# Gated delta rule on one core: the halves of x ahead of the mask constants, a large clear later, and six filter panels computed with channels on the partitions

## The chip, the cores and the metric

The kernel runs on one core of a Trainium2 chip. The time is device microseconds of one execution, the median of several runs. The core has a matrix engine (PE, TensorE; its weight loads are shown apart as PEld), a vector engine (DVE), a scalar engine (ACT), GpSimd (POOL) and a queue engine (SP) that here mostly issues the loads.

## The reference, cut to what matters

The program is one block of a small model on 256 tokens of width 1024: a gated delta rule mixer, a feed-forward layer, an S5 mixer, two mixtures of experts and per-layer embeddings. Only the first is touched:

```python
def gdn_mixer(x, w_in, conv_w, a_log, dt_bias, norm_g, w_out):
    proj = x @ w_in                                       # 256 x 1024 by 1024 x 4112
    qkv, z, b, a = jnp.split(proj, [...], axis=-1)        # q, k, v, z of 1024 columns, b and a of 8
    qkv = jax.nn.silu(causal_dwconv(qkv, conv_w))         # 4 taps along the tokens, for each channel
    q = l2norm(q) * (GDN_DK ** -0.5); k = l2norm(k)       # 8 heads of 128
    beta = jax.nn.sigmoid(b)
    g = -jnp.exp(a_log) * jax.nn.softplus(a + dt_bias)
    o = gated_delta_rule_chunked(q, k, v, g, beta)        # needs the inverse of (I + L) in each chunk
    o = o * lax.rsqrt(jnp.mean(o * o, -1, keepdims=True) + NORM_EPS) * norm_g
    return (o * jax.nn.silu(z)).reshape(bsz, seq, GDN_V) @ w_out
```

## The kernel before, in words

**The projection.** x is turned to have its 1024 features on the partitions and split into two halves whose sum is x: ACT writes `xh` (the high half), DVE `xl` (what is left). w_in is loaded by SP in pieces of 1 MiB (`raw`, five buffers); each 128x1024 slice of a piece is split the same way into `hi` (ACT, line 182) and `lo` (DVE, line 196) in three buffers. A product is then three matmuls, hi times xh, lo times xh, hi times xl (lines 204 to 206). First come the 16 columns of b and a (`sp`, 256 columns wide), then eight panels of 512 columns in the order k0, k1, q0, q1, v0, v1, z0, z1. `dense` keeps x as the stationary operand and streams 512 columns of weights, so a panel is 48 matmuls 512 wide into two PSUM banks (`mm`, four buffers) with tokens on the partitions.

**The filter.** For the six panels of k, q and v (`conv4`) ACT copies both banks to `pr` (line 498), PE turns them by eight transposes (line 503) into `tr` banks with channels on the partitions, ACT scales a copy (`cv`, line 505), and DVE adds the three other taps (line 507, three of them for each of four channel tiles). The z panels are not filtered.

**The inverse.** From k's panels LT is made (line 526); its 16x16 diagonal blocks go by SP through DRAM to `B`, DVE solves them in 15 steps (lines 572 and 574) and copies the result (`X`, line 575), and SP spreads X over the block diagonal of `DD` (lines 577 and 582), which must have been cleared (line 532). Then PE, ACT and DVE double the size of the inverted blocks: for each of two halves, three levels and two quarters, PE forms a product (line 601), ACT copies it (`pb`, line 603), PE multiplies (line 611, at the last level 607), DVE writes it under a mask (`lm`, line 612 or 608) and, but for the last level, PE turns the result (line 615) for ACT to copy (line 616). Each step needs the one before. The masks are made from a bitwise xor of two index tiles (`fi`, `pi`, `xf`).

**Order.** The instructions of an engine run in the order in which the program lists them. That list is made by a scheduler from the written order and from priorities; each instruction waits for its data by semaphores. So the matmuls of later panels that the list has between two steps of the inverse are what PE does while it waits for ACT and DVE there. What comes behind the mixer (feed-forward, S5, experts) has the same order on every engine in both kernels, from w_out's product on.

Of the kernel before, what the change touches and what calls it, by code (L numbers as in the profile page):

```python
# [6 lines left out]
F32 = mybir.dt.float32  # L7
F32R = mybir.dt.float32r
U8 = mybir.dt.uint8
I32 = mybir.dt.int32  # L10
U32 = mybir.dt.uint32
AF = mybir.ActivationFunctionType
ALU = mybir.AluOpType
# [3 lines left out]
P = 128  # L17
D = 1024
NT = 2
KD = 8  # L20
# [41 lines left out]
def behind(tc, ins, first):  # L62

    tc.add_manual_dep(ins.ins, first.ins.name, mybir.DependencyInfo(mybir.DependencyClass.NoSync, mybir.DependencyReason.DATA), reason="order")
# [13 lines left out]
class Net:  # L78
# [129 lines left out]
    def dense(self, xh, xl, w, k0, kn, n0, n, ps, first=True, last=True, then=None, lag=0):  # L208
# [27 lines left out]
        for go in late:  # L236
            go(1)

    def to_T(self, xs, xh, xl, gain=None, kt=KD, view=None, pin=False):

        nc = self.nc
        T = Pinned(self.tc, nc.tensor) if pin else nc.tensor
        done = []
        for k in range(0, kt, 2):
            n = min(2, kt - k)
            ps = self.tr()
            for j in range(n):
                for b in range(NT):
                    T.transpose(ps[:, (j * 2 + b) * P:(j * 2 + b + 1) * P], xs[b][:, (k + j) * P:(k + j + 1) * P], self.ident)  # L249
            for j in range(n):  # L250
                sl = slice(k + j, k + j + 1)
                h, l = xh[:, sl, :], xl[:, sl, :]
                v = ps[:, j * 256:(j + 1) * 256]
                if view is not None:
                    h, l = view(h)[:, 0], view(l)[:, 0]
                    v = v.rearrange("p (b j s) -> p b j s", b=2, s=4)
                else:
                    h, l = h[:, 0], l[:, 0]
                if gain is None:
                    if view is None:  # L260
                        if j == 0:
                            m = slice(k, k + n)
                            a = ps[:, :n * 256].rearrange("p (a b) -> p a b", a=n)
                            c = nc.scalar.copy(xh[:, m, :], a)
                            d = nc.vector.tensor_tensor(out=xl[:, m, :], in0=a, in1=xh[:, m, :].bitcast(F32), op=ALU.subtract)
                            done.append((c, d))
                    else:
                        nc.scalar.copy(h, v)
                        nc.vector.tensor_tensor(out=l, in0=v, in1=h.bitcast(F32), op=ALU.subtract)
                else:  # L270
                    g = gain[:, sl]
                    nc.scalar.activation(h, v, AF.Copy, scale=g)
                    nc.vector.scalar_tensor_tensor(out=l, in0=v, scalar=g, in1=h.bitcast(F32), op0=ALU.mult, op1=ALU.subtract)
        return done
# [123 lines left out]
    def gdn(self, pool, xs, outs):  # L398
        nc, i = self.nc, self.i
        V, A, T, G = nc.vector, nc.scalar, nc.tensor, nc.gpsimd  # L400
        H = 8
        w = i["gdn_w_in"]

        def t(shape, name, dt=F32, bufs=1):
            return pool.tile(shape, dt, tag=name, name=self.nm(name), bufs=bufs)


        cw = t([P, 24, 4], "cw"); nc.scalar.dma_start(cw, i["gdn_conv_w"])
# [9 lines left out]
        mneg = t([P, P], "mneg")  # L418
        G.memset(mneg, 0.0)
        G.affine_select(out=mneg, in_=mneg, pattern=[[1, P]], compare_op=ALU.is_ge, fill=-1e30, base=0, channel_multiplier=-1)  # L420
        fi = t([P, P], "fi", I32); G.iota(fi, pattern=[[1, P]], base=0, channel_multiplier=0)
        pi = t([P, P], "pi", I32); G.iota(pi, pattern=[[0, P]], base=0, channel_multiplier=1)
        V.tensor_tensor(out=fi, in0=fi, in1=pi, op=ALU.bitwise_xor)
        xf = t([P, P], "xf"); V.tensor_copy(xf, fi)
        lm = t([P, 7, P], "lm", U8)
        for l in range(4, 7):
            V.tensor_scalar(out=pi.bitcast(F32), in0=xf, scalar1=float(1 << l), scalar2=None, op0=ALU.is_ge)
            V.scalar_tensor_tensor(out=lm[:, l, :], in0=xf, scalar=float(2 << l), in1=pi.bitcast(F32), op0=ALU.is_lt, op1=ALU.mult)
        i2 = t([40, H], "i2"); sel = t([40, H, P], "sel", F32R)
        V.tensor_tensor(out=i2, in0=self.ident[:40, 0:8], in1=self.ident[:40, 32:40], op=ALU.add)  # L430
        G.tensor_copy(sel, i2.unsqueeze(2).to_broadcast([40, H, P]))
# [2 lines left out]
        xh, xl = self.xT()  # L434
# [18 lines left out]
        s8 = slice(32, 40)  # L453
# [8 lines left out]
        p0 = self.tr()  # L462
# [3 lines left out]
        p0 = self.tr()  # L466
# [4 lines left out]
        p0 = self.tr()  # L471
        for b in range(NT):
            T.matmul(p0[0:8, b * P:(b + 1) * P], gt[:, b, :], tri, start=True, stop=True)
        rw = t([40, 256], "rw", F32R)
        G.memset(rw.bitcast(F32), 0.0)
        A.copy(rw[0:8], p0[0:8, :256])
        V.tensor_tensor(out=rw[s8], in0=p0[0:8, :256], in1=rw[0:8].bitcast(F32), op=ALU.subtract)

        qT = t([P, H, 256], "qT"); kT = t([P, H, 256], "kT")
        vb = self.zt().rearrange("p b (h d) -> p b h d", h=H)  # L480
# [1 line left out]
        p0 = self.tr()  # L482
# [4 lines left out]
        def panel(n0):  # L487
            ps = [self.mm() for _ in range(NT)]
            self.dense(xh, xl, w, 0, KD, n0, 512, ps)
            return ps  # L490

        def conv4(n0, dst):

            ps = panel(n0)
            pr = [t([P, 512], "pr", bufs=3) for _ in range(NT)]
            to = []
            for b in range(NT):
                A.copy(pr[b], ps[b])
            for j in range(4):
                ct = n0 // P + j  # L500
                pt = self.tr()
                for b in range(NT):
                    T.transpose(pt[:, b * P:(b + 1) * P], pr[b][:, j * P:(j + 1) * P], self.ident)
                cv = t([P, 256], "cv", bufs=4)
                A.activation(cv, pt[:, :256], AF.Copy, scale=cw[:, ct, 3:4])
                for d in range(1, 4):
                    V.scalar_tensor_tensor(out=cv[:, d:], in0=pt[:, :256 - d], scalar=cw[:, ct, 3 - d:4 - d], in1=cv[:, d:],
                                           op0=ALU.mult, op1=ALU.add)
                to.append(cv if dst is None else dst(j))
                A.activation(to[j], cv, AF.Silu)  # L510
            return to

        def sumsq(src, n, dst):

            ps = self.tr()
            for j in range(4):
                sq = t([P, 256], "sq", bufs=2)
                G.tensor_tensor(out=sq, in0=src[:, 4 * n + j, :], in1=src[:, 4 * n + j, :], op=ALU.mult)
                for b in range(NT):
                    T.matmul(ps[:, b * 4 + j:b * 4 + j + 1], sq[:, b * P:(b + 1) * P], ones[:, 0:1], start=True, stop=True)  # L520
            V.tensor_copy(dst[:, :, 4 * n:4 * n + 4], ps[:, :8].rearrange("p (b h) -> p b h", b=NT))
# [7 lines left out]
        E = t([P, H, 384], "E"); LT = t([P, H, 384], "LT")  # L529
        B = t([P, 16, 16], "B"); X = t([P, 2, 16, 16], "X"); tp = t([P, 16, 16], "tp")  # L530
        DD = t([P, 2, 16, P], "DD")
        G.memset(DD, 0.0)
        G.memset(X, 0.0)
        G.memset(X[:, 0].rearrange("p a b -> p (a b)")[:, 0:256:17], 1.0)
        if "s5_log_dt1" in i:
# [13 lines left out]
        for n in range(2):  # L549
# [14 lines left out]
            for r in range(8):  # L564
                s = slice(16 * r, 16 * r + 16)
# [5 lines left out]
        for r in range(1, 16):  # L571
            V.tensor_tensor(out=tp[:, 0:r, 0:r], in0=X[:, 0, 0:r, 0:r].rearrange("p j n -> p n j"),
                            in1=B[:, 0:r, r].unsqueeze(1).to_broadcast([P, r, r]), op=ALU.mult)
# [4 lines left out]
        for n in range(2):  # L578
            for r in range(8):
                s = slice(16 * r, 16 * r + 16)  # L580
# [48 lines left out]
        for n in range(2):  # L629
            vT = conv4(2048 + 512 * n, None)  # L630
            for j in range(4):
                h = 4 * n + j
                pt = self.tr()
# [5 lines left out]
        for n in range(2):  # L639
            ps = panel(3072 + 512 * n)  # L640
# [1402 lines left out]
```

## Time and profile before

| what | us |
|---|---|
| runs | 1688.21, 1681.74, 1687.71 |
| median | 1687.71 |
| profiled execution | 1682.82 |
| its span in the trace | 1681.1 |
| PE busy in the span | 1545.4 (92%) |
| DVE busy | 720.7 (43%) |
| ACT busy | 489.9 (29%) |

The span is the time from the first to the last instruction of the profiled execution; 1.7 us lie around it. The mixer is the first stage. The shares of busy time are averages over the whole program; in the mixer DVE is far busier than 43%.

### The profile page before, as it was taken

How to read it: one execution, taken by the hardware profiler on the slowest of the kernel's cores; microseconds unless marked ns; L12 is line 12 of the kernel's file. 1: busy time of each engine (PE TensorE's matmuls, PEld its weight loads, DVE VectorE, ACT ScalarE, POOL GpSimd, SP SyncE). 2: the span in 40 equal slices, each digit the busy share in tenths (PEclk: the TensorE clock that was granted, in tenths of full speed). 3: DMA queues.
4: the chain of work that ended last, by engine and by line, in shares of the span. 5: the costliest groups of instructions: out<-in, count | busy, mean ns of one | idle time of the engine just before them, and what ended most of it. 6: DMA issues, size and time to landing. Idle time of an engine off the chain costs nothing. (4 is left out here: it accounts for less than half of the span.)

```text
span 1681.1 us, 25494 instructions
## 1 busy us (share of the span) xinstructions
PE 1545.4 (92%) x10438; PEld 946.0 (56%) x10438; DVE 720.7 (43%) x1334; ACT 489.9 (29%) x821; POOL 293.8 (17%) x432
## 2 busy tenths in 40 slices
PE   7999987879978979999999997988999999999997
PEld 5778866667877944544445545874443343443436
DVE  6884678757677541111111117562322222222216
ACT  5565454335542521100101014451111111111116
POOL 2201169768364000000000004000000000000000
PEclk9999999889978979999999998998999999999998
DMA  6334253774864739999899997857999999999972
GB/s 231 108 110 153 73 180 87 254 244 156 275 217 138 264 108 378 344 342 340 316 339 350 345 333 265 275 166 280 393 392 395 394 392 394 397 392 392 397 269 88
DMA packets 213567, 460.93 MB, mean 274 GB/s; under 512 B 24384, under 2 KB 63184, under 8 KB 213184
## 3 DMA queue, kind: packets, MB, share of 16 engines
q1 hardware_dynamic: 201904, 444.47, 73.7%
q0 software_dynamic: 3456, 13.07, 2.3%
q10 hardware_dynamic: 8080, 1.65, 0.5%
q8 instruction: 86, 1.41, 0.3%
q14 instruction: 41, 0.34, 0.1%
HBM read 449.18 MB, written 9.96 MB: 273 GB/s over the span
## 5 line engine op out<-in xcount | busy, mean ns | idle before, releaser
L205 PE MATMUL mm<-lo,xh 128*128 128x512 f32 (+1 forms) x632 | 233.2, 369 | 26.4 <-DVE lo L196 26.4
L196 DVE TENSOR_TENSOR lo<-raw,hi 128x1024 fp32r<-128x1024 f32 x166 | 208.1, 1260 | 108.2 <-ACT hi L182 106.4
L1811 PE MATMUL mm<-raw,xg 128*64 128x512 f32 x952 | 245.3, 601 | 2.9 <-PEq L1290 2.9
L204 PE MATMUL mm<-hi,xh 128*128 128x512 f32 (+1 forms) x632 | 234.6, 373 | 10.9 <-ACT xh L361 5.4
L206 PE MATMUL mm<-hi,xl 128*128 128x512 f32 (+1 forms) x632 | 233.4, 370 | 7.7 <-DVE xl L362 4.9
L182 ACT CAST hi<-raw 128x1024 fp32r<-128x1024 f32 x167 | 173.7, 1043 | 189.5 <-PE mm L206 138.4
L1450 PE MATMUL mm<-raw,xg 128*64 128x192 f32 (+1 forms) x1024 | 171.2, 468 | 2.8 <-PEq L1290 2.8
L205 PEld LDWEIGHTS mm<-lo,xh 128*128 128x128 f32 x632 | 123.5, 195 | 46.5 <-DVE lo L196 30.3
L1811 PEld LDWEIGHTS mm<-raw,xg 128*64 128x64 f32 x952 | 71.4, 137 | 129.0 <-issue 123.0
L204 PEld LDWEIGHTS mm<-hi,xh 128*128 128x128 f32 x632 | 123.0, 195 | 31.2 <-ACT xh L361 6.6
L206 PEld LDWEIGHTS mm<-hi,xl 128*128 128x128 f32 x632 | 122.9, 195 | 28.4 <-DVE xl L362 7.2
L1840 PE MATMUL mm<-raw,ab 128*64 128x512 f32 x480 | 132.4, 596 | 0.7 <-DVE ab L1829 0.7
L1450 PEld LDWEIGHTS mm<-raw,xg 128*64 128x64 f32 x1024 | 71.2, 137 | 91.1 <-issue 86.3
L1492 PE MATMUL mm<-raw,hT 128*32 128x256 f32 x2112 | 117.7, 380 | 0.0
L1818 DVE COPY ab<-mm 64x512 f32<-64x512 f32 x32 | 22.2, 694 | 176.6 <-ACT ab L1817 176.6
L1492 PEld LDWEIGHTS mm<-raw,hT 128*32 128x32 f32 x2112 | 67.5, 110 | 44.2 <-DMA raw<-in_moe_w_dram 0.5
L1454 PE MATMUL mm<-raw,xg 128*32 128x192 f32 (+1 forms) x1024 | 85.7, 464 | 0.0
L1499 POOL CAST y<-y 32x256 fp32r<-32x256 f32 x48 | 19.2, 413 | 380.0 <-ACT y L1280 378.1
L1840 PEld LDWEIGHTS mm<-raw,ab 128*64 128x64 f32 x480 | 44.5, 137 | 66.2 <-issue 62.2
L1817 ACT ACTIVATE ab<-mm 64x512 f32<-64x512 f32 x32 | 18.9, 590 | 210.5 <-PE mm L1811 210.5
L1515 DVE SCALAR_TENSOR_TENSOR zt<-sp,gates,zt 128x512 f32<-128x512 f32 x32 | 22.6, 747 | 121.5 <-PE sp L1513 121.4
L1854 DVE SCALAR_TENSOR_TENSOR y<-mm,gs,y 128x512 fp32r<-128x512 f32 x32 | 24.0, 751 | 86.9 <-ACT y L1853 86.6
(615 smaller groups left out, 2176.2 us busy)
## 6 DMA issues: line engine op xcount, KB each, us to landing
raw<-in_moe_w_dram SPq DMA_DIRECT2D x104, 1024.0 KB
raw<-in_w_gate_dram SPq DMA_DIRECT2D x60, 1024.0 KB
raw<-in_w_down_dram SPq DMA_DIRECT2D x60, 1024.0 KB
raw<-in_w_up_dram SPq DMA_DIRECT2D x59, 1024.0 KB
raw<-in_ffn_w_dram SPq DMA_DIRECT2D x31, 1024.0 KB
raw<-in_moe_w_dram SPq DMA_DIRECT2D x32, 768.0 KB
raw<-in_gdn_w_in_dram SPq DMA_DIRECT2D x16, 1024.0 KB
raw<-in_w_in_dram SPq DMA_DIRECT2D x10, 1024.0 KB
```

The costliest lines, as they stand in the source:

```text
L182: c = self.nc.scalar.copy(h, v)
L196: c = self.nc.vector.tensor_tensor(out=l, in0=v, in1=h.bitcast(F32), op=ALU.subtract)
L204: t.matmul(ps, lh, wh, start=first, stop=False)
L205: t.matmul(ps, lh, wl, start=False, stop=False)
L206: self.product = t.matmul(ps, ll, wh, start=False, stop=last)
L1450: T.matmul(to(p, 64 * x, 64), xg[:, k0 + k, 0:64], cols(v[z], k, x), start=k0 + k == 0, stop=k0 + k == KD - 1)
L1454: T.matmul(to(pt, 64 * z + 32 * x, 32), xg[:, k0 + k, 64:96], cols(v[z], k, x), start=k0 + k == 0, stop=k0 + k == KD - 1)
L1492: T.matmul(ps[n][32 * u:32 * u + 32], hT[:, q + f, 32 * c:32 * c + 32], v[:, f, 256 * x:256 * x + 256], start=q + f == 0, stop=q + f == 10)
L1515: V.scalar_tensor_tensor(out=a, in0=pz, scalar=gates[:, b, e:e + 1], in1=a, op0=ALU.mult, op1=ALU.add)
L1811: T.matmul(pa[64 * x:64 * x + 64, :], xg[4 * q + k][:, e % GE, :], v[x][:, k, :], start=q + k == 0, stop=q == 1 and k == 3)
L1840: T.matmul(py[n][64 * x:64 * x + 64, :], hT[x][:, 2 * q + k, :], v[x][:, k, 512 * n:512 * n + 512], start=q + k == 0, stop=q + k == 2)
L1854: V.scalar_tensor_tensor(out=yl[:, n], in0=py[n], scalar=g, in1=yh[:, n].bitcast(F32), op0=ALU.mult, op1=ALU.subtract)
```

## The change

Three edits. The mask constants are made later, behind the operation called `early`. The clear of DD (128x4096) is issued on POOL behind the fourth square of the first k panel, no longer at the start. And the six filter panels use a new function `dense_T`: the weights' 128 columns are the stationary operand and the 256 tokens of x stream, so a panel is 96 matmuls 256 wide, with channels on the partitions at once; the copies to `pr` and the transposes go, and the filter reads the `mm` banks themselves.

```diff
+    def dense_T(self, xh, xl, w, n0, n, ps):
+        kc, g = 2048 // n, 1024 // n
+        for k in range(0, KD, kc):
+            m = min(kc, KD - k)
+            v = self.load(w[k * P:(k + m) * P, n0:n0 + n].rearrange("(k p) n -> p k n", p=P), m, n)
+            for j0 in range(0, m, g):
+                h, l = self.split(v[:, j0:j0 + g, :], g, n)
+                self.tick()
+                for j in range(g):
+                    q = k + j0 + j
+                    for c in range(n // P):
+                        s = slice(c * P, (c + 1) * P)
+                        self.mm3(ps[c // 2][:, c % 2 * 256:c % 2 * 256 + 256], h[:, j, s], l[:, j, s], xh[:, q, :], xl[:, q, :],
+                                 q == 0 and c % 2 == 0, q == KD - 1 and c % 2 == 1)
...
-        fi = t([P, P], "fi", I32); G.iota(fi, pattern=[[1, P]], base=0, channel_multiplier=0)
-        pi = t([P, P], "pi", I32); G.iota(pi, pattern=[[0, P]], base=0, channel_multiplier=1)
-        V.tensor_tensor(out=fi, in0=fi, in1=pi, op=ALU.bitwise_xor)
-        xf = t([P, P], "xf"); V.tensor_copy(xf, fi)
-        lm = t([P, 7, P], "lm", U8)
-        for l in range(4, 7):
-            V.tensor_scalar(out=pi.bitcast(F32), in0=xf, scalar1=float(1 << l), scalar2=None, op0=ALU.is_ge)
-            V.scalar_tensor_tensor(out=lm[:, l, :], in0=xf, scalar=float(2 << l), in1=pi.bitcast(F32), op0=ALU.is_lt, op1=ALU.mult)
...
-        V.tensor_tensor(out=rw[s8], in0=p0[0:8, :256], in1=rw[0:8].bitcast(F32), op=ALU.subtract)
+        early = V.tensor_tensor(out=rw[s8], in0=p0[0:8, :256], in1=rw[0:8].bitcast(F32), op=ALU.subtract)
+        fi = t([P, P], "fi", I32); G.iota(fi, pattern=[[1, P]], base=0, channel_multiplier=0)
+        pi = t([P, P], "pi", I32); G.iota(pi, pattern=[[0, P]], base=0, channel_multiplier=1)
+        behind(self.tc, V.tensor_tensor(out=fi, in0=fi, in1=pi, op=ALU.bitwise_xor), early)
+        xf = t([P, P], "xf"); V.tensor_copy(xf, fi)
...
         def conv4(n0, dst):
-            ps = panel(n0)
-            pr = [t([P, 512], "pr", bufs=3) for _ in range(NT)]
+            ps = [self.mm() for _ in range(NT)]
+            self.dense_T(xh, xl, w, n0, 512, ps)
             to = []
-            for b in range(NT):
-                A.copy(pr[b], ps[b])
             for j in range(4):
                 ct = n0 // P + j
-                pt = self.tr()
-                for b in range(NT):
-                    T.transpose(pt[:, b * P:(b + 1) * P], pr[b][:, j * P:(j + 1) * P], self.ident)
+                pt = ps[j // 2][:, j % 2 * 256:j % 2 * 256 + 256]
                 cv = t([P, 256], "cv", bufs=4)
-                A.activation(cv, pt[:, :256], AF.Copy, scale=cw[:, ct, 3:4])
+                A.activation(cv, pt, AF.Copy, scale=cw[:, ct, 3:4])
...
-                G.tensor_tensor(out=sq, in0=src[:, 4 * n + j, :], in1=src[:, 4 * n + j, :], op=ALU.mult)
+                x = G.tensor_tensor(out=sq, in0=src[:, 4 * n + j, :], in1=src[:, 4 * n + j, :], op=ALU.mult)
+                if j == 3 and clear:
+                    behind(self.tc, G.memset(clear[0], 0.0), x)
+                    clear.pop()
...
-        G.memset(DD, 0.0)
+        clear = [DD]
```

The lists of the engines move with it. On PE, before, the second level of the inverse's first half stands like this among the panels (`mm<-` rows are the 512-wide matmuls of z0, `sp<-DD,LT` starts a step of the inverse, lines 601 to 615):

```order
470 L206 MATMUL mm_1468<-hi_1506,xl_131 128x512
471 L204 MATMUL mm_1468<-hi_1506,xh_130 128x512
472 L205 MATMUL mm_1468<-lo_1507,xh_130 128x512
473 L615 MATMUL sp_719<-ident,DD_244 128x128 x4
474 L601 MATMUL sp_725<-DD_244,LT_240 128x128 x4
475 L206 MATMUL mm_1468<-hi_1506,xl_131 128x512
476 L204 MATMUL mm_1469<-hi_1506,xh_130 128x512
477 L205 MATMUL mm_1469<-lo_1507,xh_130 128x512
478 L206 MATMUL mm_1469<-hi_1506,xl_131 128x512
479 L204 MATMUL mm_1469<-hi_1506,xh_130 128x512
480 L611 MATMUL sp_732<-pb_730,DD_244 128x128 x4
```

In the changed kernel the same steps (now lines 617, 627 and 631) stand in z1, the last panel, whose last matmul is here:

```order
785 L631 MATMUL sp_802<-ident,DD_244 128x128 x4
786 L617 MATMUL sp_808<-DD_244,LT_240 128x128 x4
787 L205 MATMUL mm_1735<-lo_1789,xh_116 128x512
788 L206 MATMUL mm_1735<-hi_1788,xl_117 128x512
789 L627 MATMUL sp_815<-pb_813,DD_244 128x128 x4
790 L631 MATMUL sp_821<-ident,DD_244 128x128 x4
791 L617 MATMUL sp_827<-DD_244,LT_240 128x128 x4
792 L627 MATMUL sp_834<-pb_832,DD_244 128x128 x4
793 L631 MATMUL sp_840<-ident,DD_244 128x128 x4
794 L617 MATMUL sp_846<-DD_244,LT_240 128x128 x4
```

Counted over the whole lists, 77 panel matmuls 512 wide stood behind the inverse's first product before, and 21 stand behind it now; of the 48 transposes of the filter 4 stood behind it, of the 16 transposes of line 635 eight.

On DVE, at the start of the program, `xl` stood behind the masks:

```order
3 L423 TENSOR_TENSOR fi_112<-fi_112,pi_114 128x128
4 L424 CAST xf_117<-fi_112 128x128
5 L427 TENSOR_SCALAR pi_114<-xf_117 128x128
6 L428 SCALAR_TENSOR_TENSOR lm_119<-xf_117,pi_114 128x128
7 L427 TENSOR_SCALAR pi_114<-xf_117 128x128
8 L428 SCALAR_TENSOR_TENSOR lm_119<-xf_117,pi_114 128x128
9 L427 TENSOR_SCALAR pi_114<-xf_117 128x128
10 L428 SCALAR_TENSOR_TENSOR lm_119<-xf_117,pi_114 128x128
11 L265 TENSOR_TENSOR xl_131<-tr_132,xh_130 128x512
12 L265 TENSOR_TENSOR xl_131<-tr_139,xh_130 128x512
```

Now it is DVE's fourth instruction:

```order
2 L438 TENSOR_TENSOR i_112<-ident 40x8
3 L281 TENSOR_TENSOR xl_117<-tr_118,xh_116 128x512
4 L281 TENSOR_TENSOR xl_117<-tr_125,xh_116 128x512
5 L453 TENSOR_TENSOR balo_149<-wba_146,bahi_148 128x8x8 x2
6 L196 TENSOR_TENSOR lo_307<-raw_304,hi_306 128x1024
7 L281 TENSOR_TENSOR xl_117<-tr_132,xh_116 128x512
8 L281 TENSOR_TENSOR xl_117<-tr_139,xh_116 128x512
```

Further down the list of DVE the copy of X (line 575, now 591) stood behind 22 splits `lo` and stands behind 26 now, and the eight mask operations stand between the first rows of E, ahead of the seventh split.

On SP the spreading of X over DD stood ahead of all loads of w_out:

```order
22 L171 DMA raw_1578<-in_gdn_w_in_dram 128x4x512
23 L577 DMA dX<-X_242 128x512
24 L582 DMA DD_244<-dX 16x8x16 x32
25 L171 DMA raw_1828<-in_gdn_w_out_dram 128x4x512
26 L171 DMA raw_1862<-in_gdn_w_out_dram 128x4x512
```

Now two of these loads are issued ahead of it and a third between its two steps:

```order
22 L171 DMA raw_1770<-in_gdn_w_in_dram 128x4x512
23 L171 DMA raw_2020<-in_gdn_w_out_dram 128x4x512
24 L171 DMA raw_2054<-in_gdn_w_out_dram 128x4x512
25 L593 DMA dX<-X_242 128x512
26 L171 DMA raw_2090<-in_gdn_w_out_dram 128x8x256
27 L598 DMA DD_244<-dX 16x8x16 x32
28 L171 DMA raw_2154<-in_gdn_w_out_dram 128x8x256
```

## Rows read from the trace of the kernel before

**Rows 1.** One 20 us stretch: busy us (instructions) of PE, PEld, DVE, ACT, POOL, PE's clock.

```profile
100.00:120.00 20.00, 19.15 (x99) 14.99 (x99) 18.34 (x48) 10.55 (x22) 1.20 (x2) 1.00 0.24 71
```

**Rows 2.** Timeline of the start: start us, duration us, instruction, count, idle time before.

```profile
5.03 5.85 DVE L424 CAST xf<-fi 128x128 f32<-128x128 int32 x1
6.82 3.50 POOL L532 MEMSET DD<- 128x4096 f32 x1
8.37 1.07 ACT L264 CAST xh<-tr 128x512 fp32r<-128x512 f32 x2
10.32 1.04 ACT L182 CAST hi<-raw 128x1024 fp32r<-128x1024 f32 x1 [0.59 <-DMA raw<-in_gdn_w_in_dram]
12.56 1.28 DVE L265 TENSOR_TENSOR xl<-tr,xh 128x512 fp32r<-128x512 f32 x2
13.30 1.11 PE L249 MATMUL tr<-ident,x 128*128 128x128 f32 x4 [5.35 <-DVE xl L265]
17.26 0.39 PE L204 MATMUL mm<-hi,xh 128*128 128x512 f32 x1
```

**Rows 3.** Timeline of PE: 256-wide matmuls and a weight load, then 512-wide ones.

```profile
17.73 0.28 PE L205 MATMUL sp<-xl,bahi 128*128 128x256 f32 x1
...
18.77 0.19 PEld L206 LDWEIGHTS sp<-xh,balo 128*128 128x128 f32 x1
18.88 0.28 PE L206 MATMUL sp<-xh,balo 128*128 128x256 f32 x1
...
123.62 0.39 PE L204 MATMUL mm<-hi,xh 128*128 128x512 f32 x1
...
125.00 0.40 PE L204 MATMUL mm<-hi,xh 128*128 128x512 f32 x1
```

**Rows 4.** Groups of instructions of the first 200 us: busy us, mean ns.

```profile
L196 DVE TENSOR_TENSOR lo<-raw,hi 128x1024 fp32r<-128x1024 f32 x38 | 46.4, 1227 | 18.4 <-ACT hi L182 17.5 <-PE mm L206 0.8
L507 DVE SCALAR_TENSOR_TENSOR cv<-tr,cw,cv 128x255 f32<-128x255 f32 (+2 forms) x72 | 30.5, 474 | 0.5 <-ACT cv L505 0.3
L503 PE MATMUL tr<-ident,pr 128*128 128x128 f32 x48 | 9.2, 279 | 0.4 <-DVE cv L507 0.3
```

**Rows 5.** Timeline of PE around one group of the filter's transposes.

```profile
127.96 0.60 PE L503 MATMUL tr<-ident,pr 128*128 128x128 f32 x4
...
128.63 0.39 PE L204 MATMUL mm<-hi,xh 128*128 128x512 f32 x1
```

**Rows 6.** Timeline of PE, the waits behind the sixth split.

```profile
44.00 0.73 PE L204 MATMUL mm<-hi,xh 128*128 128x512 f32 x2 [0.71 <-ACT hi L182]
46.35 0.50 PE L205 MATMUL mm<-lo,xh 128*128 128x512 f32 x1 [0.69 <-DVE lo L196]
```

**Rows 7.** Timeline from the copy of X to the inverse's first product.

```profile
112.65 0.37 DVE L575 COPY X<-X 128x256 f32<-128x256 f32 x1
...
125.23 1.05 PE L601 MATMUL sp<-DD,LT 128*128 128x128 f32 x8
```

**Rows 8.** Timeline of the inverse: starts of steps on PE, and the last masked write.

```profile
139.17 1.06 PE L601 MATMUL sp<-DD,LT 128*128 128x128 f32 x8
...
143.45 1.06 PE L601 MATMUL sp<-DD,LT 128*128 128x128 f32 x8
...
146.23 1.06 PE L601 MATMUL sp<-DD,LT 128*128 128x128 f32 x8
...
149.02 1.06 PE L601 MATMUL sp<-DD,LT 128*128 128x128 f32 x8
...
171.48 1.06 PE L601 MATMUL sp<-DD,LT 128*128 128x128 f32 x8
...
174.53 0.73 DVE L608 COPY_PREDICATED DD<-lm,sp 128x512 f32<-128x512 uint8 x1 [2.12 <-PE sp L607]
```

**Rows 9.** Timeline of DVE and PE, the longest wait of PE in the mixers.

```profile
284.91 9.10 DVE L59 TENSOR_TENSOR zt<-half,vk 128x16 f32<-128x16 f32 x1
...
297.08 0.79 PE L205 MATMUL mm<-lo,xh 128*128 128x512 f32 x1 [10.74 <-DVE lo L196]
```

More of the change, by code (lines that the diff above doesn't have):

```diff
@@ L476, in gdn @@
         A.copy(rw[0:8], p0[0:8, :256])
-        V.tensor_tensor(out=rw[s8], in0=p0[0:8, :256], in1=rw[0:8].bitcast(F32), op=ALU.subtract)
+        early = V.tensor_tensor(out=rw[s8], in0=p0[0:8, :256], in1=rw[0:8].bitcast(F32), op=ALU.subtract)
[3 more added lines that the diff above has]
+        xf = t([P, P], "xf"); V.tensor_copy(xf, fi)
+        lm = t([P, 7, P], "lm", U8)
+        for l in range(4, 7):
+            V.tensor_scalar(out=pi.bitcast(F32), in0=xf, scalar1=float(1 << l), scalar2=None, op0=ALU.is_ge)
+            V.scalar_tensor_tensor(out=lm[:, l, :], in0=xf, scalar=float(2 << l), in1=pi.bitcast(F32), op0=ALU.is_lt, op1=ALU.mult)
         qT = t([P, H, 256], "qT"); kT = t([P, H, 256], "kT")
```

## The prediction, as put on record before the changed kernel ran

> **What bounds the kernel now.** I read the busy shares first (PE 92%), and then, because these hide stages with other limits, the busy time by stretches of 20 us over the mixer. In the panels two engines are nearly full at once: between 100 and 120 us PE is busy 19.15 us and DVE 18.34 of 20 [rows 1]. So PE's work bounds the stage, but a microsecond taken from PE is only kept where DVE's splits `lo` (1.23 us each), taps (0.47 us each) [rows 4] and steps of the small solve come in time. ACT, at 10.55 us, has room. Next the timeline of the start: PE waits 5.35 us for `xl`, which DVE gets to at 12.56 because a cast of 5.85 us stands ahead of it, beside POOL's clears [rows 2]. Then the timeline of the inverse: from its first product at 125.23 [rows 7] to the last masked write, which ends at 174.53 + 0.73 = 175.26 [rows 8], each step waits for the one before on another engine, and PE fills the gaps with panel matmuls. There the chain sets the pace, and not PE's total.
>
> The whole question is thus when the inverse ends. Behind it the lists are the same, so that what the mixer gains or loses is carried to the end.
>
> **The start.** Without the masks ahead of it `xl` needs only `xh`, whose first two casts run from 8.37 to 9.44 [rows 2]. It could run at about 9.0, 3.6 us earlier. The gain is between 0 (if the first weights are late) and 5.35 (PE's whole wait). The first weights are late only a little: the cast `hi` waits for its DMA until 10.32, so its `lo` can be had at about 10.32 + 1.04 + 1.23 = 12.6, against the first panel matmul at 17.26 now. I take 4 us. Behind the start PE comes sooner to small operations that wait for DVE, so some of this may be lost again; the DVE time of the masks, 8 instructions, isn't saved but moved between the rows of E, except for what the cast lost to its neighbours (all but some 0.3 us of 5.85, if the clears were the cause).
>
> **The matmuls.** A panel of `dense_T` has 96 matmuls 256 wide in place of 48 that are 512 wide. Eleven 256-wide ones start between 17.73 and 18.88, 0.115 us apart; seven of 512 between 123.62 and 125.00, 0.23 us apart [rows 3]. Two narrow ones cost one wide one, although a weight load takes 0.19 us in the same rows: it lies behind the matmuls before it. So 0; upper bound, if each pair had to pay its two loads in full, 288 pairs by (0.38 - 0.23) = 43 us more.
>
> The Trainium skill, TensorE: Matmul & The Clock Gate, section Back-to-back issue gap, speaks against this: weight load and matmul together set the spacing, and it gives 81 ns for 128 columns and 131 ns for 512. An estimate of 98 ns for 256 columns on a line between them would make a pair 64 ns dearer than one wide matmul, 18 us over 288 pairs. The trace doesn't agree for this type: 115 ns is half of 230.
>
> **The transposes and copies.** Four transposes start at 127.96, and the second matmul behind them at 128.63 [rows 5]: 0.67 less one 512-wide spacing of 0.23 is 0.44 us, 0.11 for one. The 48 cost 5.3 us of PE, 4.8 of it (44 of them) ahead of the inverse's first product. The twelve copies to `pr` lie on ACT, which has room; they were a delay between panel and filter and no bound. What is late next is DVE: the `mm` banks are now held until its 12 taps of a panel are done (12 by 0.47 = 5.6 us at most), and the panel after next needs them. That panel starts 48 matmuls later, 48 by 0.23 = 11 us, so it is hidden as long as DVE lags by less than 5 us. DVE's own work doesn't shrink: it has the same taps and splits.
>
> **The waits behind the sixth split.** 0.71 and 0.69 us [rows 6], where DVE is behind with the rows of E. With the start earlier and the taps not in one piece ahead of the splits they may go: 0 to 1.4. I take 1.4, since DVE gets 4 us of lead.
>
> **The clear of DD.** 3.50 us on POOL [rows 2], which is otherwise nearly idle there (1.20 of 20 us busy [rows 1]). DD is needed only when X is spread, tens of us later. The cost is 0; if it holds up a DVE operation as the clears seem to have held the cast, up to 3.5.
>
> **The cover of the inverse.** This is the part that takes. 77 panel matmuls stood behind the inverse's first product, 21 stand there now: 56 by 0.23 = 12.9 us of PE work has gone ahead of it, and eight transposes of line 635, 0.9 us. The product moves from 125.23 to 125.23 + 12.9 + 0.9 - 4 - 4.8 - 1.4 = 128.8 if PE sets it. Its data come by X's copy, 12.6 us before it now [rows 7]. That copy stands behind four more splits, 4.9 us, and the moved masks, 2 to 3 us (1.7 for the six behind the cast, from its end at 10.88 to 12.56 [rows 2], and the cast and the xor), but DVE starts 4 us sooner and loses less: 109 to 117, so the data are there at 122 to 130. About the same point, and I let PE set it.
>
> Then the chain runs nearly bare. With cover a step took up to 5 us; without, PE's starts at 139.17 and 143.45 give 4.28 for one that ends in a transpose, and 146.23 to 149.02 gives 2.79 for one of the last level [rows 8]. Both were paced by the chain, so they are its price without cover too. Eight of the first, three of the second and a last one of 175.26 - 171.48 = 3.78 [rows 8] make 34.2 + 8.4 + 3.8 = 46.4 us. The inverse ends at 128.8 + 46.4 = 175.2; now it ends at 175.26. The sum is 0.
>
> In short: 4 + 5.3 + 1.4, about 10.7 us of work and waits, are saved ahead of the inverse; 13.8 us of cover are lost, of which 50.0 - 46.4 = 3.6 come back because the steps no longer wait for panel matmuls. Against the profiled execution (1682.82, of which 1681.1 is span) that is 1683; the median of the runs shown, 1687.71, lies 5 us above it, so I put the forecast at 1684.
>
> **The rivals.**
> *The savings hold and the inverse starts early* (faster). If the start gives all of 5.35 us and DVE's lag goes with it, so that X's copy is at 109 and PE is at the product at 125 or sooner, the inverse ends at 171, and if PE's other waits shrink too, at 167: 1675 to 1679. For it: DVE's cast loses 5 us. Against: DVE is full at 18.34 of 20 us.
> *A wait elsewhere goes* (faster). At 284.91 one small DVE operation took 9.10 us beside a busy POOL, and PE waited 10.74 [rows 9]. Its neighbours take well under a microsecond, so this depends on how two engines meet. The order there is the same, but if the shift moves them apart, 10 us go: 1673.
> *The data come late* (slower). The spreading of X now stands behind a load of w_out on SP, which waits until a `raw` buffer is free, thus for a split. If X's copy comes at 117 and that load holds the 32 transfers for another 8 us, the first product comes at 117 + 12.6 + 8 = 138, 9 us later than PE gets there: 1693. It begins to cost when the copy and the wait together end after 116.2 (128.8 - 12.6), and it passes 0.5% only from some 13 us on.
> *The narrow matmuls cost more* (slower): 18 to 43 us, thus 1701 to 1726, from the price above. The rows speak against it.
> *DVE holds the banks*: a lag of over 5 us behind the panel's end makes PE wait at each of four panels, some 2 us each: 1691.
>
> **How the numbers follow.** 0.5%, 8.4 us, is what a measurement of this kernel can tell from no change: faster is below 1679.3, slower above 1696.1. The forecast (gains and lost cover cancel, 1680 to 1689) has 0.48. The savings hold: 0.18. The wait elsewhere goes: 0.10. The data late: 0.10, the banks: 0.08, narrow matmuls dear: 0.04, the remaining 0.02 anything worse. The range: 1672 takes in both faster cases, 1694 the late data and the banks; outside stay the dear matmuls and the far ends of the others. Faster: the savings and the wait, with a little of the forecast's edge, 0.30. Slower: the matmuls, the rest and the worst of the late data and of the banks, 0.12. Same: 0.58.
>
> **What would show it.** In the timeline `xl` near 9 us and the first panel matmul near 13. In the groups 288 by 2 matmuls of 256 columns, 0.115 apart. The first product of the inverse at 127 to 131, then steps of 4.28 us with PE idle for about half of each, waiting for ACT's copies and DVE's masked writes; the last masked write near 175. If the product comes before 126 the savings were larger than I think; if PE waits there for DMA, the data are late; if PE waits at a panel's first matmul for taps, the banks are. The forecast is wrong if the steps take other than 4.28 and 2.79 without cover, or if DVE, and not PE, sets the place of the product.

## The result, and the profile of the changed kernel

The changed kernel takes 1696.17 us (median of 8 runs) against 1683.62 us of the kernel before (8 runs): a ratio of 1.008, 95% interval 1.0064 to 1.0095, slower by 0.8%. The forecast was 1684 with a range of 1672 to 1694. The profiled execution has a span of 1697.2 us, 16.1 more than before. Single executions carry a difference in the mixer to their end only roughly: from the last masked write to the end of the span it takes 1502 to 1511 us in the profiles used here, so the ratios decide.

The start went as the diff says. In the timeline `xl` runs at 8.82 where it ran at 12.56, and the first panel matmul at 14.11 where it stood at 17.26 [rows 2]:

```profile
8.82 1.29 DVE L281 TENSOR_TENSOR xl<-tr,xh 128x512 fp32r<-128x512 f32 x2 [6.10 <-ACT xh L280]
9.57 1.12 PE L265 MATMUL tr<-ident,x 128*128 128x128 f32 x4 [1.76 <-DVE xl L281]
...
14.11 0.41 PE L204 MATMUL mm<-xh,hi 128*128 128x256 f32 x1
```

The panels behind it did not keep the lead. PE's waits in the timeline of the first 50 us, and two matmuls between them that are ten spacings apart:

```profile
24.90 0.26 PE L472 MATMUL tr<-ident,gr 8*128 8x8 f32 x2 [1.86 <-DVE gr L468]
...
29.98 0.41 PE L204 MATMUL mm<-xh,hi 128*128 128x256 f32 x1
...
32.12 0.41 PE L205 MATMUL mm<-xl,hi 128*128 128x256 f32 x1
...
45.51 0.38 PE L206 MATMUL mm<-xh,lo 128*128 128x256 f32 x1 [1.70 <-DVE lo L196]
```

The columns of the next view are busy us (instructions) of PE, PEld, DVE, ACT, POOL, then the clock granted to PE, DMA share and GB/s:

```profile
20.00:24.00 4.00, 3.04 (x27) 2.83 (x25) 2.89 (x4) 2.26 (x5) 0.00 (x0) 1.00 1.01 370
24.00:26.00 2.00, 1.10 (x8) 1.11 (x9) 1.69 (x3) 0.99 (x1) 0.00 (x0) 0.92 0.94 225
26.00:32.00 6.00, 6.00 (x30) 5.37 (x29) 2.43 (x7) 1.41 (x2) 0.00 (x0) 0.50 0.27 106
32.00:36.00 4.00, 4.00 (x28) 3.49 (x28) 2.77 (x13) 1.82 (x3) 0.00 (x0) 0.94 0.79 239
36.00:44.00 8.00, 7.82 (x51) 6.32 (x49) 5.57 (x21) 5.96 (x10) 0.00 (x0) 1.00 0.03 13
44.00:46.00 2.00, 0.49 (x4) 0.49 (x5) 2.00 (x4) 0.90 (x4) 0.00 (x0) 1.00 0.00 0
46.00:50.00 4.00, 4.00 (x24) 4.00 (x23) 2.95 (x5) 2.54 (x5) 0.62 (x1) 0.57 0.46 105
```

PE waits 1.86 us for `gr`, and behind it the granted clock is 0.50 (1.2 in place of 2.4 GHz) until past 32 us; it waits 1.70 us for a split, and the mean clock between 46 and 50 us is 0.57. PE reads as fully busy in both stretches. Only the spacing tells: 2.14 us over ten spacings, 0.214 us for one, where such a matmul costs 0.118 at the full clock (timeline of PE; 21 spacings lie between these two):

```profile
76.48 0.28 PE L205 MATMUL mm<-xl,hi 128*128 128x256 f32 x1
...
78.95 0.28 PE L205 MATMUL mm<-xl,hi 128*128 128x256 f32 x1
```

Two narrow matmuls thus still cost one wide one (0.23 [rows 3]).

In the kernel before the wait for `gr` was half as long. By the timelines its transposes stood behind 39 wide panel matmuls there, and stand behind 60 narrow ones now, the work of 30 wide ones:

```profile
28.62 0.26 PE L464 MATMUL tr<-ident,gr 8*128 8x8 f32 x2 [0.90 <-DVE gr L460]
```

The next rows are the chain to the inverse, from the timelines of DVE, SP and PE; the rows that answer to them are [rows 7], [rows 8] and, for LT, the one below:

```profile
83.11 1.51 DVE L542 SCALAR_TENSOR_TENSOR LT<-sp,cn,E 128x256 f32<-128x256 f32 x4 [1.07 <-PE sp L575]
...
126.07 0.37 DVE L591 COPY X<-X 128x256 f32<-128x256 f32 x1
...
130.46 16.93 SPq L598 DMA_DIRECT2D DD<-dX  x32
...
142.21 1.05 PE L617 MATMUL sp<-DD,LT 128*128 128x128 f32 x8
...
151.35 1.06 PE L617 MATMUL sp<-DD,LT 128*128 128x128 f32 x8
155.61 1.06 PE L617 MATMUL sp<-DD,LT 128*128 128x128 f32 x8
...
162.65 1.06 PE L617 MATMUL sp<-DD,LT 128*128 128x128 f32 x8
...
165.43 1.06 PE L617 MATMUL sp<-DD,LT 128*128 128x128 f32 x8
...
188.31 0.73 DVE L624 COPY_PREDICATED DD<-lm,sp 128x512 f32<-128x512 uint8 x1 [2.07 <-PE sp L623]
```

```profile
73.36 1.63 DVE L526 SCALAR_TENSOR_TENSOR LT<-sp,cn,E 128x256 f32<-128x256 f32 x4 [0.38 <-PE sp L559]
```

X is copied at 126.07, 13.4 us later than before, and the inverse's first product is at 142.21, 17.0 later. No idle time stands before that product, and PE is busy 20.00 of the 20 us from 120 to 140: PE came to it late and did not wait there for its data. From there the steps run bare, 4.26 and 2.78 us each, and the last masked write ends at 189.04, 13.8 later than the 175.26 before. The rest of the program follows: the long wait of [rows 9] is there again, 10.90 us long, at 311.13 in place of 297.08.

Where PE's time went shows in two stretches, from the first panel matmul to the inverse's first product and from there to the end of the last masked write. The first two rows are the kernel before, the others the changed kernel (columns as above):

```profile
17.26:125.23 107.97, 104.55 (x522) 81.57 (x521) 85.57 (x202) 66.51 (x115) 13.64 (x16) 1.00 0.43 128
125.23:175.26 50.03, 48.45 (x332) 41.56 (x331) 23.00 (x33) 26.72 (x51) 5.10 (x4) 1.00 0.41 129
```

```profile
14.11:142.21 128.10, 120.02 (x830) 109.65 (x830) 98.27 (x223) 71.14 (x122) 20.02 (x19) 0.96 0.46 142
142.21:189.04 46.83, 36.56 (x264) 31.45 (x264) 13.76 (x20) 18.30 (x32) 2.55 (x2) 1.00 0.22 70
```

Ahead of the product PE stood idle 3.42 us before and 8.08 now (the stretch less PE's busy time), and the clock that fell short of 1.00 cost 5.1 us (0.04 of 128.10), where it cost nothing. Besides `gr` and the split, PE now waits four times, 2.6 us in all, for POOL's squares of k. Behind the product its idle time rose from 1.58 to 10.27 us.

### The profile page after: what moved, and what is told of

Same layout as the page of the kernel before. It is cut to its first block, busy times and chain, and to the rows that moved or that the text cites. A ratio compares the mean times of both kernels' runs of the same rounds, so it can differ in the third digit from the quotient of the medians.

```text
span 1697.2 us, 25969 instructions
## 1 busy us (share of the span) xinstructions
PE 1550.7 (91%) x10678; PEld 964.0 (57%) x10678; DVE 717.8 (42%) x1334; ACT 484.8 (29%) x809; POOL 295.4 (17%) x432
## 5 line engine op out<-in xcount | busy, mean ns | idle before, releaser
L205 PE MATMUL mm<-lo,xh 128*128 128x512 f32 (+1 forms) x536 | 193.5, 361 | 25.5 <-DVE lo L196 25.5
L204 PE MATMUL mm<-hi,xh 128*128 128x512 f32 (+1 forms) x536 | 194.5, 364 | 9.4 <-ACT xh L377 5.4
L206 PE MATMUL mm<-hi,xl 128*128 128x512 f32 (+1 forms) x536 | 192.7, 361 | 5.9 <-DVE xl L378 3.2
L205 PEld LDWEIGHTS mm<-lo,xh 128*128 128x128 f32 x536 | 104.7, 195 | 42.6 <-DVE lo L196 28.9
L204 PEld LDWEIGHTS mm<-hi,xh 128*128 128x128 f32 x536 | 104.5, 195 | 26.9 <-ACT xh L377 6.6
L206 PEld LDWEIGHTS mm<-hi,xl 128*128 128x128 f32 x536 | 103.9, 194 | 23.5 <-DVE xl L378 5.6
```

What stands on the lines that cost most here:

```text
L204: t.matmul(ps, lh, wh, start=first, stop=False)
L205: t.matmul(ps, lh, wl, start=False, stop=False)
L206: self.product = t.matmul(ps, ll, wh, start=False, stop=last)
```

## The experiments

All are ratios to the kernel before, timed on the same chip with 95% intervals. "Product" is the start of the inverse's first product, "end" the end of its last masked write, in the profiled execution.

**Which of the three edits.** One alone, or one undone. The first two lists are those of the kernel before on PE; the third is the changed kernel's.

```diff
 e1_masks:    kernel before, mask constants behind early
 e2_clear:    kernel before, DD's memset behind the fourth square
 e3_T:        kernel before + dense_T in conv4
 e4_T_masks:  changed kernel, G.memset(DD, 0.0) back at its old place
```

> The kernel before with the mask constants made later and nothing else. Every list is the one of before but for DVE's first rows; 307 panel matmuls stay ahead of the inverse's first product. Theory A (the loss comes with the list that dense_T brings): the start gains about 3 us and loses some of it at the small transposes of gr, so 0 to 3 us faster, inverse product at 122 to 125 us. Theory B (the earlier start itself loses: PE waits 2 us for gr, the clock falls to its lower level behind the wait, and the panels come later): a clock below 1.00 between 25 and 35 us and 0 to 4 us slower than before.

> The kernel before with the clear of DD behind the fourth square and nothing else. Theory A: no change, within 2 us; with the clear gone from the start the cast of the masks may lose part of its 5.85 us, which would give 1 to 3 us. Theory C (the clear holds DVE and the squares of k in the middle of the chain to the inverse): k's LT and the copy of X come 2 to 4 us later than in the kernel before (112.65 us), and so does the inverse's first product, 0 to 4 us slower.

> The kernel before with dense_T and nothing else. 363 panel matmuls stand ahead of the inverse's first product, as in the changed kernel. Theory A: nearly the whole loss, 10 to 14 us slower, the inverse's first product at 138 to 143 us. Theory B and C: the loss needs the earlier start or the late clear, so 3 us slower at most, product at 132 us or sooner, no clock below 1.00 in the panels.

> The changed kernel with the clear of DD back at the start (dense_T and the later masks stay). Theory C: 2 to 4 us faster than the changed kernel, the copy of X at 122 to 124 us in place of 126.07, no DVE operation of 2 us near 61 us. Theory A: the same as the changed kernel within 2 us, since PE's list and not the data places the inverse's first product.

| kernel | ratio | interval | product, us | end, us |
|---|---|---|---|---|
| masks alone | 0.9991 | 0.9974 to 1.0008 | 124.74 | 174.76 |
| clear alone | 0.9981 | 0.9961 to 1.0001 | 128.98 | 179.00 |
| dense_T alone | 1.0087 | 1.0065 to 1.0109 | 143.42 | 190.20 |
| dense_T and masks | 1.0061 | 1.0038 to 1.0084 | 140.10 | 186.88 |

dense_T alone brings the whole loss. The masks alone gain the start and keep nothing that can be measured. The late product of the clear alone belongs to the execution that was profiled, which took 1685.21 us, where the median is 1679.43, and ran at a mean clock of 0.57 between 28 and 40 us. The long wait for `gr` comes with dense_T's list, and not with the earlier start, as PE shows with the masks alone and with dense_T alone:

```profile
25.67 0.26 PE L456 MATMUL tr<-ident,gr 8*128 8x8 f32 x2 [0.88 <-DVE gr L452]
```

```profile
28.02 0.29 PE L480 MATMUL tr<-ident,gr 8*128 8x8 f32 x2 [1.86 <-DVE gr L476]
```

Whether the late clear costs time beside dense_T is not shown: 1.0061 without it and 1.008 with it have overlapping intervals, and most of the 2.1 us between the two products is the clock between 20 and 40 us, 0.91 and 0.83. That the clear holds an operation is shown by the changed kernel's timeline, POOL and DVE:

```profile
59.54 3.52 POOL L533 MEMSET DD<- 128x4096 f32 x1
...
60.93 2.16 DVE L569 TENSOR_SCALAR brk<-brk 128x8 f32<-128x8 f32 x1
61.00 2.10 DVE L520 SCALAR_TENSOR_TENSOR cv<-mm,cw,cv 128x255 f32<-128x255 f32 x1
```

An operation on 128x8 that takes 0.16 us at its next place (76.93) is held until the clear ends, in the chain to k's LT. The Trainium skill, SBUF — State Buffer, section Who interferes with whom, has copies, casts and tensor_scalar among those that, with operands that allow it, can be blocked by GpSimd for a whole instruction; the trace agrees, 2.16 us beside the clear.

**The order of the filter.** In ACT's list of the changed kernel the fourth channel tile of k1 (`cv_640`) and its Silu (`kT` from `cv_640`) have the first tile of the next panel, q0, between them (`cv_1092`, which needs all of q0):

```
54 L518 ACTIVATE cv_640<-mm_505,cw_94 128x256
55 L182 CAST hi_1186<-raw_1156 128x1024
56 L518 ACTIVATE cv_1092<-mm_974,cw_94 128x256
57 L182 CAST hi_1216<-raw_1214 128x1024
58 L523 ACTIVATE kT_229<-cv_640 128x256
```

ACT's timeline shows the wait of that row for PE, and k's Silu behind it:

```profile
68.13 0.46 ACT L518 ACTIVATE cv<-mm,cw 128x256 f32<-128x256 f32 x1
...
72.38 0.47 ACT L518 ACTIVATE cv<-mm,cw 128x256 f32<-128x256 f32 x1 [1.90 <-PE mm L206]
...
73.93 0.41 ACT L523 ACTIVATE kT<-cv 128x256 f32<-128x256 f32 x1
```

On DVE, too, the scheduler put splits between a tile's three taps, each of which needs the one before. The remedy tried is the same work written two (or four) tiles at a time:

```diff
-            for j in range(4):
-                ... cv of tile j; its taps d = 1, 2, 3; its Silu
+            for g in range(0, 4, 2):
+                ... cv of tiles g and g + 1
+                for d in range(1, 4):
+                    ... tap d of tile g, tap d of tile g + 1
+                ... the two Silus
```

> The changed kernel with the clear of DD at the start and the filter's taps written two channel tiles at a time, the same instructions in another order: 308 panel matmuls stand ahead of the inverse's first product, the copy of X behind 22 splits, and ACT's list has a panel's four tiles together. Theory D (the loss is the order of the filter: tile by tile, a panel's last tile stands behind the next panel's end in ACT's list, so that k's LT, X and the inverse come late): LT of k1 done at 75 us or sooner, the copy of X at 108 to 113, the inverse's first product at 118 to 124, and 1672 to 1680 us, some 15 us less than the kernel with both (1692.72). Theory E (dense_T's matmuls themselves, with PE's waits for gr and the lower clock behind them, are the loss): no more than 4 us less, 1688 to 1693.

> As the one with pairs, but all four channel tiles of a panel written together (307 panel matmuls ahead of the product). Theory D: within 3 us of it. Theory E: 1688 to 1693.

> The changed kernel complete, clear of DD late too, with the taps in pairs. Theory C (the late clear holds DVE and the squares in the chain to the inverse): LT of k1 2 to 4 us later than with the clear at the start and 2 to 4 us more than that kernel. Theory D without C: the same within 1.5 us.

And with the banks freed by ACT's copies as before, tile by tile:

> The changed kernel with the clear at the start and with ACT's two copies of each panel kept (of the banks into pr, then the filter from pr, tile by tile as in the change). The banks come free as before and 292 panel matmuls stand ahead of the product. If the held banks were the cause: 1672 to 1682 us like the pairs, with the copies' 7 us of ACT time hidden. If only the order of the tiles mattered and copies cost the chain time: 2 to 4 us more than the pairs. Theory E: 1688 to 1693.

| kernel | ahead | ratio | interval | product, us | end, us |
|---|---|---|---|---|---|
| pairs, early clear | 308 | 1.0027 | 1.001 to 1.0045 | 131.93 | 181.48 |
| pairs, late clear | 308 | 1.0024 | 1.0006 to 1.0042 | 127.07 | 176.62 |
| fours, early clear | 307 | 1.01 | 1.0072 to 1.0128 | 146.16 | 193.48 |
| copies, early clear | 292 | 1.0103 | 1.0078 to 1.0127 | 144.98 | 193.56 |

The order of the pairs takes off more than half of the loss, but not all that theory D wanted (1672 to 1680), and D fell for the fours and the copies: there the list looks as wanted and the time, 1700.73 and 1700.46 us, lies above all that was expected of them. Their windows show the clock: 0.66 and 0.67 between 40 and 60 us, below 1.00 in nearly every stretch of 20 us until 140, and PE waits 6.1 and 9.0 us in all for the squares of k on POOL. A list that is right in the count of matmuls can still make PE wait elsewhere.

What the pairs bring is seen in the two stretches of PE, here with the late clear:

```profile
14.31:127.07 112.76, 104.88 (x767) 98.25 (x766) 90.31 (x219) 62.92 (x106) 14.43 (x17) 0.95 0.43 134
127.07:176.62 49.55, 48.20 (x327) 40.84 (x326) 20.32 (x25) 25.20 (x48) 5.13 (x4) 1.00 0.42 130
```

Ahead of the product PE's idle time (7.88 us) and its clock are much as in the changed kernel (8.08); behind it PE stands idle 1.35 us in place of 10.27, since 55 more wide matmuls are there to cover the steps. Between the two kernels with pairs the clear makes no difference that can be measured, against theory C.

**PE's waits and the clock.** First `gr`'s transposes alone were moved six matmuls down PE's list, then the small products of `gt` too, with all else in place:

```diff
+  if q == 5: the transposes of gr behind this product        (g1, g2, g4; j1 and j2)
+  if q == 6: the products of gt behind this product          (j1 and j2)
```

> The changed kernel with one order more: the two transposes of gr stand six panel matmuls later in PE's list (36 in place of 30), everything else where it was (363 ahead of the inverse's first product). Theory F (PE's wait of 1.86 us for gr brings the clock to its lower level, and the half speed behind it costs as much again or more): no wait over 0.6 us at gr, granted clock 1.00 between 24 and 34 us, the first panel some 4 us sooner, and 2 to 4 us faster than the changed kernel (1696.17). If the clock has no part in it: within 1.5 us of the changed kernel, since the wait itself only moves.

> The changed kernel with the taps in pairs (308 ahead of the product) and with gr's transposes six matmuls later. Theory F with D (lost cover and the clock are two separate parts): 2 to 4 us less than pairs alone (1688.41), 1684 to 1686. If the pairs alone already had no loss at gr: no change from 1688.

> The changed kernel, taps tile by tile, with gr's transposes later and with ACT's two copies kept for the first k panel alone, so that its banks come free while DVE is with the rows of E (323 ahead of the product, the copy of X behind 22 splits). Theory G (PE's wait for k0's banks, 2.6 us at 43 us in the kernels with pairs, and the clock behind it): no wait for taps at q0's first matmul, clock 1.00 from 40 to 60 us, 1680 to 1686 us. If the splits behind the taps hold PE in its place: a wait for lo of 2 to 5 us near 42 us with a lower clock behind it, 1688 to 1694.

> The changed kernel with gr's transposes behind the sixth k tile of the first panel and the next small products (of gt) behind the seventh, the list otherwise the same (363 ahead of the inverse's first product). If waits and the lower clock at the start cost total time: clock 1.00 from 20 to 40 us, product at 137 to 139 us, and 3 to 5 us less than the changed kernel on the same chip. If what follows takes it back: within 1.5 us of it.

> The same two delays with the taps in pairs (308 ahead of the product). If the clock at the start costs: clock 1.00 from 20 to 40 us, and 2 to 4 us less than pairs alone (1.0024 to 1.0027 of the kernel before), so level with the kernel before or just below it. The wait of 2.6 us for k0's banks near 43 us, with the lower clock behind it, stays in any case.

> The changed kernel itself, beside the three others on the same chip: 1.008 of the kernel before, the inverse's first product at 139 to 143 us.

| kernel | ratio | interval | median, us | product, us | end, us |
|---|---|---|---|---|---|
| gr later | 1.0095 | 1.0075 to 1.0115 | 1697.91 | 139.08 | 185.92 |
| pairs, gr later | 1.0021 | 1.0003 to 1.0039 | 1686.39 | 127.46 | 177.01 |
| copies for k0, gr later | 1.0067 | 1.0049 to 1.0085 | 1694.14 | 139.77 | 186.99 |
| changed kernel again | 1.0084 | 1.0059 to 1.0109 | 1697.41 | 141.61 | 188.46 |
| gr and gt later | 1.0063 | 1.004 to 1.0086 | 1692.18 | 136.71 | 183.55 |
| pairs, gr and gt later | 1.0017 | 1.0 to 1.0033 | 1683.37 | 125.83 | 175.38 |

The last three ran on one chip. `gr` alone was a miss: the wait went, but the next one, 0.81 us for `gt`, stood behind it, the clock fell there too, and the time did not move, although the end of the inverse came 2.5 us sooner in its profile (185.92 and 188.46). With both moved the clock stays up. Windows of the changed kernel taken again, then of the one with both moved (columns as above):

```profile
20.00:40.00 20.00, 18.14 (x104) 16.11 (x103) 11.31 (x32) 9.06 (x13) 0.00 (x0) 0.74 0.54 184
```

```profile
20.00:40.00 20.00, 19.20 (x136) 16.55 (x134) 14.96 (x44) 12.05 (x19) 0.00 (x0) 1.00 0.55 184
```

In the same 20 us PE issues 136 instructions in place of 104. The product comes 4.9 us sooner and the medians differ by 5.2 us, with the same 363 matmuls ahead of the product. The two intervals of the ratios overlap, and by the ratios the difference is 3.5 us (0.21%). The profiles say that the clock made most of it: between the first panel matmul and the product the changed kernel lost 5.1 us to the half clock and this one none, and 0.8 us was gained before (first panel matmul at 13.44 and 14.20). The waits hardly shrank in sum (8.09 and 7.85 us): one of 1.94 us for a split stands where one of 1.69 was. Against this PE's own work came out 1.2 us longer, for which no row gives a reason. X's copy came sooner by as much as the product, 120.59 and 125.47.

With the pairs as well the end of the inverse is at 175.38, and before it was 175.26. In that kernel one long wait is left, at q0's first matmul for k0's taps, and the clock behind it is low (timeline and windows):

```profile
41.67 0.55 PE L204 MATMUL mm<-xh,hi 128*128 128x256 f32 x1 [2.84 <-DVE cv L530]
```

```profile
40.00:60.00 20.00, 17.79 (x99) 17.02 (x100) 13.97 (x32) 6.71 (x14) 5.98 (x5) 0.66 0.33 97
```

The attempt to free those banks by copies for k0 alone had the wait replaced by others, 3.6 us for the squares at one place. That price stays unmeasured.

**Without dense_T.** Both other edits together, and the same with `gr` later:

> The kernel before with the later masks and the later clear, without dense_T, in its old list (307 ahead of the product). If the start's gain is kept: 2 to 5 us below the kernel before, 0.997 to 0.999 of it. If it is lost at the next wait for DVE: 0.999 to 1.001.

> The kernel before with the later masks, the later clear and gr's transposes six matmuls later in PE's list, without dense_T (305 ahead of the product). If these two edits gain what the start shows and dense_T alone loses: unit 0 at 14 to 15 us in place of 17.26, product at 121 to 125 us, 1676 to 1681 us, below the kernel before (1683 to 1684). If the start's gain is lost at the next wait for DVE: within 2 us of the kernel before.

They gave 1.0 (0.9985 to 1.0016) and 1.0011 (0.9998 to 1.0024), with first panel matmuls at 13.9 and 14.7 us and the product at 126.38 and 127.17. The 3 us of the start are lost again before the inverse: PE waits 1.5 and 2.1 us for a tap near 43 and 45 us, where its longest wait there had been 0.7 us, and the clock between 40 and 60 us is 0.91. No version beat the kernel before by more than the noise.

## Why the prediction was wrong

The step that failed is the sum that places the inverse's first product, "125.23 + 12.9 + 0.9 - 4 - 4.8 - 1.4 = 128.8 if PE sets it". PE did set it, at 142.21: it came there without a wait. Term by term, from the stretches shown with the result (work is PE's busy time less what the half clock cost):

| term, us | forecast | measured |
|---|---|---|
| the start | -4 | -3.15 |
| work ahead of the product (12.9 + 0.9 - 4.8) | +9.0 | +10.3 |
| PE's waits ahead of the product | -1.4 | +4.7 |
| PE's clock | 0, not named | +5.1 |
| sum | +3.6 | +17.0 |

The start and the transposes were won nearly as forecast. But the prediction took over PE's waits from the old list, less 1.4 us, and did not ask for its clock; new waits and half clock, 9.8 us, took back most of the 10.7 that it counted as saved.

- **The start**: 3.15 us gained, 4 forecast. Right, but "some of this may be lost again" was priced at nothing. The first loss is 1.86 us at `gr` and the half clock behind it; the runs lay it to dense_T's list, which has `gr` behind fewer matmuls, and not to the earlier start.
- **The matmuls**: right. 0.118 against 0.115 us, and no weight load shows. The rule of the Trainium skill's page TensorE: Matmul & The Clock Gate, section Back-to-back issue gap (by the prediction's estimate 18 us more) did not hold for this type: all of PE's work ahead of the product came out 1.3 us over the sum.
- **The waits behind the sixth split**: "I take 1.4" gained; in its place one wait of 1.70 us came, and in one of the two profiles of the changed kernel another stretch at half clock. DVE did not get its lead: the first of E's rows needs the small products behind `gr`, made at half clock, and came at 33.74, where it came at 33.01 before (with `gr` and `gt` moved and the clock up, at 29.73); the first taps are at 43.85, and were at 42.75.
- **The clear**: 0 forecast, 3.5 as the bound. It held an operation for 2 us; a cost in the total is not shown, beside the tile by tile filter or beside the pairs.
- **The cover**: right in mechanism. From the product to the last masked write it took 46.8 us, 46.4 forecast, by steps of 4.26 and 2.78.
- **The data**: "109 to 117, so the data are there at 122 to 130". X was copied at 126.07, 9 us beyond the late end. I counted the splits ahead of X's copy (26) and the masks, and not what k's filter itself waits for: its tiles stand in ACT's and DVE's lists among those of the next panel, so LT of k1 was done at 84.6 where it had been done at 75.0. Had PE come at 128.8, it would have waited: 126.07 and the 12.6 us of the kernel before make 138.7 (an estimate). PE and the data were late together, DVE splits what PE multiplies, and no run parts the two.
- **The rivals**: "the data come late" was near in time, but PE's place, and not a wait for data, is what the trace shows at the product. SP's load between the two steps of X's spreading cost about 2 us of the data's time (4.4 from the copy to the spreading, 2.5 before). "DVE holds the banks" was seen only in the kernels with pairs, 2.6 to 2.8 us at one panel, and with fours, 4.2. The wait at 285 us did not go.

The sum, on one chip, is 0.84% by the ratios: 0.21% goes with `gr` and `gt` moved, which takes the half clock at the start away; 0.46% goes with the order of the taps; 0.17% remains, with an interval that reaches 0. By the medians it is 5.2, 8.8 and 0.4 us. The first of these differences is hardly clear of the noise, the second is. The pairs bring X sooner and leave 308 matmuls ahead of the product and the others to cover the steps, which is where PE's idle time went; the earlier data are what lets the product stand there, and no run here tells the two apart. The transposes that were taken out, 5.3 us by rows, buy nothing in the end: level with the kernel before at best.

## What to carry to other kernels

Work taken from a busy engine is a gain only where the chain behind it comes sooner; find the operation that the chain starts from, and follow its inputs through every engine's list, before adding up what is saved. A new list brings new waits: count how much work it leaves ahead of each small operation that waits for another engine, and do not take the old waits over into the sum. Where a scheduler makes the list, a chain of dependent steps written one after the other lets other work in between its steps; written interleaved, the same work came out some 8 us sooner in pairs and no sooner in fours, and only a run told which. And a wait of PE is worth more than its length when the clock falls behind it, so read the granted clock of short windows, since the busy share shows nothing.

## What the hardware showed that was not expected

- The length of a wait of PE alone does not decide whether the clock falls. In one profile of the changed kernel waits of 1.86 and 1.70 us were followed by some 7 and 3 us at half clock; in the other 1.86 us was followed by half clock until past 34 us, and 1.69 us by none. 0.90 us left the clock at 1.00 in the kernel before, while in the profile of the late clear alone a wait of 0.88 us was followed by that mean clock of 0.57. And with `gr` and `gt` moved a wait of 1.94 us left the clock at 1.00 behind it (timeline and windows):

```profile
41.51 0.39 PE L206 MATMUL mm<-xh,lo 128*128 128x256 f32 x1 [1.94 <-DVE lo L196]
```

```profile
44.00:48.00 4.00, 4.00 (x34) 3.66 (x33) 2.95 (x8) 2.81 (x5) 0.61 (x1) 1.00 0.88 262
```

- A clear on POOL holds DVE's cast for its whole length. The cast of the masks took 5.85 us with all clears beside it [rows 2], 2.40 with DD's clear of 3.50 us gone, and 0.23 us in the changed kernel, where no clear ran.
